# Left operands of the seven products made two products ahead, and the input's quarter sums from a float32 copy

## The chip, the cores and the metric

The kernel runs on one core of a Trainium2 chip, as one launch. The engines of a core run their own instruction queues in order and meet through semaphores: TensorE (PE: matmuls; PEld: its loads of the left operand), VectorE (DVE), ScalarE (ACT), GpSimd (POOL) and SyncE (SP), which issues the weight loads. The metric is the device time of one execution in microseconds (us). Three runs of the kernel before took 1692.21 us in the median, 1684.16 to 1693.19.

## The reference

One inference step of a two-layer decoder trunk over 544 tokens: 512 tokens of one prompt and 8 sequences of 4 tokens. Layer 0 is a convolution module and a SwiGLU feed-forward network (FFN). Layer 1 is sparse attention, over keys and values projected once, and a second SwiGLU FFN. Each part is normalised, then scaled and shifted by a vector per sequence. The change is in the FFN of layer 1:

```python
def swiglu(h, w_gate, w_up, w_down):
    return (jax.nn.silu(h @ w_gate) * (h @ w_up)) @ w_down

shift, scale, gate = ada_modulation(c, w_ada[l, 1], b_ada[l, 1])
h = rmsnorm(x, norm_g[l, 1]) * (1 + scale) + shift
x = x + gate * swiglu(h, w_gate[l], w_up[l], w_down[l])
```

Here h is 544 x 1024, `w_gate` and `w_up` are 1024 x 2816, `w_down` is 2816 x 1024, all float32.

## The kernel before, in words

Activations lie with features on the 128 partitions and tokens in columns: `h` is 8 feature tiles of 128 x 544. float32 accuracy comes from splitting each operand into a high part, rounded to the type float32r, and a low part, the rest. A product of two operands takes three matmuls: high x high, high x low and low x high. ScalarE makes the high part of a weight tile (`whi`) by a cast, VectorE the low part (`wlo`) by a subtraction. `whi` and `wlo` are rings of four buffers, each of four 128 x 128 tiles, and the raw weights (`raw`) a ring of four, each of eight. A buffer comes free when the last instruction that reads it is done.

The 22 output tiles ("units") of the FFN's hidden width are done in three thirds, of 8, 8 and 6 units. In each third the gate and up products are made, then multiplied by the third's part of `w_down` and added to x. In the second FFN (line 1698, `start` is given) there are three kinds of units. Units 0 and 1 (`EARLY`) multiply the unnormalised x, so that they can start before the norm is known. Then `modulated` (line 520) makes the high and low parts of the true h, and units 2 and 3 use them plainly: we call these the whole units. From unit 4 on (`SEVEN`), units go in pairs through `seven_units` (line 881), which calls `seven` (line 222) twice, for gate and up.

One call of `seven` multiplies a 256-row block of weights (two units, two halves of the input features) by two halves of the tokens with seven half-size products instead of eight (a 2 x 2 block scheme with sums of blocks on both sides). The left operands are, in program order, a11, the sums s1, s2, the block a12, the sums s4, s3, and a22. `seven_weights` (line 198) is a generator that makes each of them when it is asked for. The right operands are three quarters of h, and four quarter sums T ("t1" to "t4"), made once for all calls by `sums_of_halves` (line 255). One product ("term", line 232) is 12 matmuls of 272 columns. Terms of one call gather in three PSUM areas (`p1`, `p2`, `p3`), of which ScalarE copies out intermediate values (lines 240, 242, 245) before the next term adds to them, and VectorE adds results (lines 247, 249, 251). The last term of a call is done only after the next call's second (`earlier`), so calls are chained. There are 9 pairs, 18 calls: 2 pairs in the first third, 4 in the second, 3 in the last.

`sums_of_halves` rebuilds h as high + low in float32 (line 261, into the ring `ht` of three buffers, which the whole units' SiLU and other temporaries use as well), forms four combinations of 272 columns (lines 264 to 267, tile `su`), and splits them into T's high part (line 269, ScalarE) and low part (line 270, VectorE). It is called for four pairs of feature tiles, two after unit 2 and two after unit 3 (line 856). GpSimd makes low parts of the hidden activations (lines 855 and 904).

The order of instructions on each engine is chosen when the kernel is built. A scheduler walks the program with its own estimate of times and takes ready instructions by their place in the program, so an operation that is written earlier tends to stand earlier. At run time each engine follows that order strictly.

Of the kernel before, what the change touches and what calls it, by code (L numbers as in the profile page):

```python
# [7 lines left out]
F32 = mybir.dt.float32  # L8
# [6 lines left out]
P = 128  # L15
D = 1024
KT = D // P
SEQ = 512
# [94 lines left out]
class Kernel:  # L113
# [83 lines left out]

    def seven_weights(self, src, pool):


        add = lambda out, x, y: self.v.tensor_tensor(out=out, in0=x, in1=y, op=ALU.add)  # L201
        a = self.wp.tile([P, KT, P], F32, name="raw", bufs=4)
        b = self.wp.tile([P, KT, P], F32, name="raw", bufs=4)
        s24 = pool.tile([P, 2, 4, P], F32, name="s24", bufs=2)
        s13 = pool.tile([P, 2, 4, P], F32, name="s13", bufs=1)
        self.sy.dma_start(a, src[:, :, :P])
        self.sy.dma_start(b, src[:, :, P:])
        av, bv = [t.rearrange("p (k c) n -> p c k n", c=2) for t in (a, b)]
        a11, a12, a22, s1, s3 = av[:, 0], av[:, 1], bv[:, 1], s13[:, 0], s13[:, 1]
        add(s1, bv[:, 0], a22)  # L210
        yield self.split4(a11)
        yield self.split4(s1)
        add(s24[:, 0], s1, a11)
        yield self.split4(s24[:, 0])
        yield self.split4(a12)
        add(s24[:, 1], s24[:, 0], a12)
        yield self.split4(s24[:, 1])
        add(s3, a11, bv[:, 0])
        yield self.split4(s3)
        yield self.split4(a22)  # L220

    def seven(self, src, X, pool, c1, c22, earlier):

# [5 lines left out]
        p1, p2 = pg[:, 0, :n], pg[:, 1, :n]  # L229
        ws = self.seven_weights(src, pool)  # L230

# [22 lines left out]

    def sums_of_halves(self, hi, lo, T, i, pool):

        v, s = self.v, self.s
        n = TOK // 2
        x = [self.tp.tile([P, TOK], F32, name="ht", bufs=3) for _ in range(2)]
        for c in range(2):  # L260
            v.tensor_tensor(out=x[c], in0=hi[:, 2 * i + c, :TOK].bitcast(F32), in1=lo[:, 2 * i + c, :TOK].bitcast(F32), op=ALU.add)
        (b11, b12), (b21, b22) = [(t[:, :n], t[:, n:]) for t in x]
        t = [pool.tile([P, TOK], F32, name="su", bufs=2).rearrange("p (a n) -> p a n", a=2) for _ in range(2)]
        v.tensor_tensor(out=t[0][:, 0], in0=b11, in1=b12, op=ALU.subtract)
        v.scalar_tensor_tensor(out=t[0][:, 1], in0=b22, scalar=-1.0, in1=t[0][:, 0], op0=ALU.mult, op1=ALU.subtract)
        v.tensor_tensor(out=t[1][:, 0], in0=b22, in1=b12, op=ALU.subtract)
        v.scalar_tensor_tensor(out=t[1][:, 1], in0=t[0][:, 1], scalar=-1.0, in1=b21, op0=ALU.mult, op1=ALU.subtract)
        for a in range(2):
            s.copy(T[0][:, i, 2 * a:2 * a + 2], t[a])
            v.tensor_tensor(out=T[1][:, i, 2 * a:2 * a + 2], in0=t[a], in1=T[0][:, i, 2 * a:2 * a + 2].bitcast(F32), op=ALU.subtract)  # L270

    def quarters(self, hi, lo, T):
        n = TOK // 2
        at = lambda x, c, a: lambda i: x[:, 2 * i + c, a * n:(a + 1) * n]
        X = {k: (at(hi, c, a), at(lo, c, a)) for k, c, a in (("11", 0, 0), ("21", 1, 0), ("22", 1, 1))}
        of = lambda x, j: lambda i: x[:, i, j]
        X.update({f"t{j + 1}": (of(T[0], j), of(T[1], j)) for j in range(4)})
        return X
# [240 lines left out]

    def modulated(self, m, rstd):  # L520

        for f in range(KT):
            self.modulated_prompt(m, f, rstd)
            if f == 0:
                self.modulated_decode(m, 0, KT, rstd)

    def modulated_prompt(self, m, f, rstd):
        a, b = self.mod[:, m, 1], self.mod[:, m, 0]
        t = self.tp.tile([P, TOK], F32, name="ht", bufs=3)
        self.v.scalar_tensor_tensor(out=t[:, :SEQ], in0=self.x[:, f, :SEQ], scalar=a[:, f, 0:1], in1=rstd[:, :SEQ],  # L530
                                    op0=ALU.mult, op1=ALU.mult)
        self.s.activation(self.h_hi[:, f, :SEQ], t[:, :SEQ], AF.Identity, bias=b[:, f, 0:1])
        self.v.scalar_tensor_tensor(out=self.h_lo[:, f, :SEQ], in0=t[:, :SEQ], scalar=b[:, f, 0:1],
                                    in1=self.h_hi[:, f, :SEQ].bitcast(F32), op0=ALU.add, op1=ALU.subtract)

    def modulated_decode(self, m, f0, f1, rstd):
# [9 lines left out]
        self.s.copy(self.h_hi[:, f0:f1, SEQ:], ts)  # L546
        self.v.tensor_tensor(out=self.h_lo[:, f0:f1, SEQ:], in0=ts, in1=self.h_hi[:, f0:f1, SEQ:].bitcast(F32), op=ALU.subtract)  # L547

    def unscaled_shift(self, m, hi, lo):
# [244 lines left out]
    def ffn(self, l, pool, between=(), done=lambda f: None, start=None):  # L794
# [15 lines left out]
        if start is not None:  # L810
            sums = self.tc.tile_pool(name="sums", bufs=1, side="right", reuse_waits="tile")
            sp = sums.__enter__()
            T = [sp.tile([P, 4, 4, TOK // 2], F32R, name=f"T{c}") for c in range(2)]
            X = self.quarters(self.h_hi, self.h_lo, T)
        for lo, hi in ((0, 8), (8, 16), (16, FT)):
            for j in range(lo, hi):
                if start is not None and j >= SEVEN:
                    if (j - lo) % 2 == 0:
                        left = self.seven_units(j, lo, gs, us, X, sp, pool, left, a_hi, a_lo)
                        for _ in range(4):  # L820
                            next(between, None)
                    continue
# [3 lines left out]
                if start is not None and j == EARLY:  # L826
                    self.modulated(m, rstd)
                if early:
# [23 lines left out]
                while units and not (early and j < EARLY - 1):  # L852
                    i, sg = j - lo + 1 - len(units), units.pop(0)
                    s.copy(a_hi[:, i], sg)  # L854
                    self.last_pool = g.tensor_tensor(out=a_lo[:, i], in0=sg, in1=a_hi[:, i].bitcast(F32), op=ALU.subtract).ins  # L855
                if start is not None and EARLY <= j < EARLY + 2:
                    for i in range(2):
                        self.sums_of_halves(self.h_hi, self.h_lo, T, 2 * (j - EARLY) + i, sp)
                next(between, None)
# [20 lines left out]

    def seven_units(self, j, lo, gs, us, X, sp, pool, left, a_hi, a_lo):

        v, s, g = self.v, self.s, self.g
        n = TOK // 2
        sg = [pool.tile([P, TOK], F32, name="early", bufs=2 * EARLY) for _ in range(2)]
        p1, last = self.seven(gs[:, :, j * P:(j + 2) * P], X, sp, sg[0], sg[1][:, n:], left)
        s.activation(sg[0], sg[0], AF.Silu)
# [8 lines left out]

        s0, s1 = self.tp.tile([P, TOK], F32, name="ht", bufs=3), sp.tile([P, TOK], F32, name="su", bufs=2)[:, :n]
        q1, end = self.seven(us[:, :, j * P:(j + 2) * P], X, sp, s0, s1, gates)
        v.tensor_tensor(out=sg[0], in0=sg[0], in1=s0, op=ALU.mult)
# [832 lines left out]
```

## Time and profile before

| | |
|---|---|
| median of three runs | 1692.21 us |
| the profiled execution | 1690.65 us |
| its span, first to last instruction | 1688.9 us |
| mean granted TensorE clock over it | 0.976 of full speed |
| TensorE busy | 1584.2 us, 94% |
| VectorE busy | 1000.5 us, 59% |
| ScalarE busy | 645.8 us, 38% |
| GpSimd busy | 231.9 us, 14% |

The second FFN's norm and whole units begin near 1281 us, the first call of `seven` near 1322 us. Its thirds end with down products near 1382 to 1426, 1523 to 1567 and from 1639 us on. In the timelines a matmul's end is modelled: matmuls overlap, and at full pace one begins about every 0.126 us while each shows 0.29 us. So time that is lost is read from start to start. "x2" is two instructions that the view merged.

### The profile page before, as it was taken

How to read it: one execution, taken by the hardware profiler on the slowest of the kernel's cores; microseconds unless marked ns; L12 is line 12 of the kernel's file. 1: busy time of each engine (PE TensorE's matmuls, PEld its weight loads, DVE VectorE, ACT ScalarE, POOL GpSimd, SP SyncE). 2: the span in 40 equal slices, each digit the busy share in tenths (PEclk: the TensorE clock that was granted, in tenths of full speed). 3: DMA queues.
4: the chain of work that ended last, by engine and by line, in shares of the span. 5: the costliest groups of instructions: out<-in, count | busy, mean ns of one | idle time of the engine just before them, and what ended most of it. 6: DMA issues, size and time to landing. Idle time of an engine off the chain costs nothing. (4 is left out here: it accounts for less than half of the span.)

```text
span 1688.9 us, 31583 instructions
## 1 busy us (share of the span) xinstructions
PE 1584.2 (94%) x12591; PEld 1388.1 (82%) x12591; DVE 1000.5 (59%) x2167; ACT 645.8 (38%) x1328; POOL 231.9 (14%) x267
## 2 busy tenths in 40 slices
PE   6889869999999999989999899999999899999997
PEld 3689337989988999989978677655699899999997
DVE  1799645473325554422657544876757865874766
ACT  4322106232122222123545332756644442552554
POOL 2146420021221111001110000000011310010010
PEclk9999978999999999999999999999999899999999
DMA  7745875374389999952379896847023372333231
GB/s 228 186 138 132 199 236 174 103 237 138 120 217 333 335 338 324 253 158 69 106 243 282 253 281 189 249 125 233 25 76 100 114 226 82 91 101 88 77 90 63
DMA packets 315326, 296.05 MB, mean 175 GB/s; under 512 B 15843, under 2 KB 275053, under 8 KB 310939
## 3 DMA queue, kind: packets, MB, share of 16 engines
q1 hardware_dynamic: 304507, 237.24, 47.6%
q0 software_dynamic: 10368, 56.56, 10.5%
q8 instruction: 99, 1.62, 0.4%
q14 instruction: 48, 0.39, 0.1%
q10 hardware_dynamic: 304, 0.23, 0.1%
HBM read 257.39 MB, written 45.76 MB: 179 GB/s over the span
## 5 line engine op out<-in xcount | busy, mean ns | idle before, releaser
L168 ACT CAST whi<-raw 128x512 fp32r<-128x512 f32 (+1 forms) x306 | 184.0, 609 | 549.1 <-PE g L184 344.5
L169 DVE TENSOR_TENSOR wlo<-raw,whi 128x512 fp32r<-128x512 f32 (+1 forms) x306 | 212.0, 696 | 228.5 <-ACT whi L168 222.9
L182 PE MATMUL g<-h_hi,whi 128*128 128x256 f32 (+1 forms) x808 | 236.7, 294 | 19.6 <-DVE un L649 8.8
L184 PE MATMUL g<-h_hi,whi 128*128 128x272 f32 (+3 forms) x808 | 239.4, 297 | 0.7 <-ACT h_hi L546 0.7
L184 PE MATMUL g<-h_lo,whi 128*128 128x272 f32 (+3 forms) x808 | 239.3, 296 | 0.4 <-DVE h_lo L547 0.4
L184 PE MATMUL g<-h_hi,wlo 128*128 128x272 f32 (+3 forms) x808 | 239.4, 296 | 0.0
L182 PE MATMUL g<-h_lo,whi 128*128 128x256 f32 (+1 forms) x808 | 233.3, 289 | 0.0
L182 PE MATMUL g<-h_hi,wlo 128*128 128x256 f32 (+1 forms) x808 | 233.0, 288 | 0.0
L182 PEld LDWEIGHTS g<-h_hi,whi 128*128 128x128 f32 x808 | 154.7, 192 | 33.7 <-issue 13.2
L184 PEld LDWEIGHTS g<-h_hi,whi 128*128 128x128 f32 x808 | 154.7, 192 | 4.6 <-issue 3.5
L182 PEld LDWEIGHTS g<-h_lo,whi 128*128 128x128 f32 x808 | 155.1, 192 | 3.7 <-issue 3.5
L184 PEld LDWEIGHTS g<-h_hi,wlo 128*128 128x128 f32 x808 | 154.5, 191 | 3.4 <-issue 3.4
L184 PEld LDWEIGHTS g<-h_lo,whi 128*128 128x128 f32 x808 | 154.2, 191 | 2.9 <-issue 2.1
L182 PEld LDWEIGHTS g<-h_hi,wlo 128*128 128x128 f32 x808 | 155.0, 192 | 1.3 <-issue 1.0
L182 PE MATMUL g<-a_hi,whi 128*128 128x256 f32 (+1 forms) x372 | 107.1, 288 | 6.2 <-ACT a_hi L854 2.7
L184 PE MATMUL g<-a_hi,wlo 128*128 128x288 f32 (+1 forms) x372 | 110.5, 297 | 0.0
L184 PE MATMUL g<-a_hi,whi 128*128 128x288 f32 (+1 forms) x372 | 110.2, 297 | 0.0
L184 PE MATMUL g<-a_lo,whi 128*128 128x288 f32 (+1 forms) x372 | 109.8, 295 | 0.0
L182 PE MATMUL g<-a_hi,wlo 128*128 128x256 f32 (+1 forms) x372 | 105.4, 284 | 0.7 <-DVE wlo L169 0.7
L182 PE MATMUL g<-a_lo,whi 128*128 128x256 f32 (+1 forms) x372 | 105.0, 282 | 0.9 <-POOL a_lo L855 0.9
L237 PE MATMUL g<-T,whi 128*128 128x272 f32 x432 | 84.0, 290 | 2.2 <-ACT early L240 2.2
L182 PEld LDWEIGHTS g<-a_hi,whi 128*128 128x128 f32 x372 | 70.7, 190 | 11.7 <-ACT whi L168 4.5
(467 smaller groups left out, 3428.1 us busy)
## 6 DMA issues: line engine op xcount, KB each, us to landing
raw<-in_w_ada_dram SPq DMA_DIRECT2D x96, 512.0 KB
raw<-in_w_gate_dram SPq DMA_DIRECT2D x44, 512.0 KB
raw<-in_w_up_dram SPq DMA_DIRECT2D x44, 512.0 KB
raw<-in_w_down_dram SPq DMA_DIRECT2D x32, 512.0 KB
raw<-in_w_pw_dram SPq DMA_DIRECT2D x24, 512.0 KB
kt_d<-ktr SPq DMA_DIRECT2D x96, 128.0 KB
kt<-kt_d SPq DMA_DIRECT2D x24, 512.0 KB
raw<-in_w_kv_dram SPq DMA_DIRECT2D x20, 512.0 KB
```

Of the source, the lines that this page charges most:

```text
L168: self.s.copy(hi[:, :b - a], raw[:, a:b])
L169: self.v.tensor_tensor(out=lo[:, :b - a], in0=raw[:, a:b], in1=hi[:, :b - a].bitcast(F32), op=ALU.subtract)
L182: self.te.matmul(pg[:, 0, :split], a, b[:, i, :split], start=st, stop=sp)
L184: self.te.matmul(pg[:, 1, :tokens - split], a, b[:, i, split:tokens], start=st, stop=sp)
L237: self.te.matmul(out, a[:, i], b(i), start=first and i == 0 and j == 0, stop=i == 3 and j == 2, skip_group_check=not first)
```

## The change

The generator `seven_weights` now runs over all weight blocks of a third (`srcs`), and `ahead` draws from it so that, whenever a product takes its operand, the two after it have already been written into the program, across calls too. The sums lie in a ring `s4` of three buffers, in place of `s13` and `s24`, and each is written directly behind the product before it.

`modulated` takes a function `whole`. For each feature tile ScalarE then also writes h in float32, without rounding (a second activation of 512 columns and a copy of 32), into a tile of the same ring `s4`. `sums_of_halves` takes that tile and forms the four combinations in place, so lines 261 and the `ht` tiles are gone from it, and it splits all four at once, 1088 columns wide. The first call of it is written before feature tile 6 of `modulated`, the other three after unit 2. T's columns are stored in another sequence (`quarters`).

```diff
-    def seven_weights(self, src, pool):
-        add = lambda out, x, y: self.v.tensor_tensor(out=out, in0=x, in1=y, op=ALU.add)
...
-        s24 = pool.tile([P, 2, 4, P], F32, name="s24", bufs=2)
-        s13 = pool.tile([P, 2, 4, P], F32, name="s13", bufs=1)
...
+    def seven_weights(self, srcs, pool):
+        def sums(x, y):
+            out = pool.tile([P, 4, TOK // 2], F32, name="s4", bufs=3).rearrange("p a n -> p (a n)")[:, :4 * P].rearrange("p (k n) -> p k n", k=4)
+            self.v.tensor_tensor(out=out, in0=x, in1=y, op=ALU.add)
+            return out
+
+        for src in srcs:
+            raws = [self.wp.tile([P, KT, P], F32, name="raw", bufs=4) for _ in range(2)]
+            for i, raw in enumerate(raws):
+                self.sy.dma_start(raw, src[:, :, i * P:(i + 1) * P])
+            (a11, a12), (a21, a22) = [[r.rearrange("p (k c) n -> p c k n", c=2)[:, c] for c in range(2)] for r in raws]
+            yield self.split4(a11)
+            s1 = sums(a21, a22)
+            yield self.split4(s1)
+            s2 = sums(s1, a11)
+            yield self.split4(s2)
+            yield self.split4(a12)
+            s4 = sums(s2, a12)
+            yield self.split4(s4)
+            yield self.split4(sums(a11, a21))
+            yield self.split4(a22)
+
+    def ahead(self, it, n):
+        made = []
+        for x in it:
+            made.append(x)
+            if len(made) > n:
+                yield made.pop(0)
+        yield from made
...
-    def sums_of_halves(self, hi, lo, T, i, pool):
+    def sums_of_halves(self, x, T, i):
...
-        x = [self.tp.tile([P, TOK], F32, name="ht", bufs=3) for _ in range(2)]
-        for c in range(2):
-            v.tensor_tensor(out=x[c], in0=hi[:, 2 * i + c, :TOK].bitcast(F32), in1=lo[:, 2 * i + c, :TOK].bitcast(F32), op=ALU.add)
...
-        for a in range(2):
-            s.copy(T[0][:, i, 2 * a:2 * a + 2], t[a])
-            v.tensor_tensor(out=T[1][:, i, 2 * a:2 * a + 2], in0=t[a], in1=T[0][:, i, 2 * a:2 * a + 2].bitcast(F32), op=ALU.subtract)
+        q = [x[:, j] for j in range(4)]
+        v.tensor_tensor(out=q[0], in0=q[0], in1=q[1], op=ALU.subtract)
+        v.tensor_tensor(out=q[1], in0=q[3], in1=q[1], op=ALU.subtract)
+        v.scalar_tensor_tensor(out=q[3], in0=q[3], scalar=-1.0, in1=q[0], op0=ALU.mult, op1=ALU.subtract)
+        v.scalar_tensor_tensor(out=q[2], in0=q[3], scalar=-1.0, in1=q[2], op0=ALU.mult, op1=ALU.subtract)
+        s.copy(T[0][:, i], x)
+        v.tensor_tensor(out=T[1][:, i], in0=x, in1=T[0][:, i].bitcast(F32), op=ALU.subtract)
...
-    def modulated(self, m, rstd):
+    def modulated(self, m, rstd, whole=None):
...
+            if whole:
+                out = whole(f)
+                self.s.activation(out[:, :SEQ], t[:, :SEQ], AF.Identity, bias=self.mod[:, m, 0, f, 0:1])
+                self.s.copy(out[:, SEQ:], ts[:, f])
...
+            xs = []
+
+            def whole(f):
+                if f == KT - 2:
+                    self.sums_of_halves(xs[0], T, 0)
+                if f % 2 == 0:
+                    xs.append(sp.tile([P, 4, TOK // 2], F32, name="s4", bufs=3))
+                return xs[-1].rearrange("p (c a) n -> p c (a n)", c=2)[:, f % 2]
         for lo, hi in ((0, 8), (8, 16), (16, FT)):
+            if start is not None:
+                ws = self.ahead(self.seven_weights((m[:, :, j * P:(j + 2) * P] for j in range(max(lo, SEVEN), hi, 2) for m in (gs, us)), sp), 2)
...
-                    self.modulated(m, rstd)
+                    self.modulated(m, rstd, whole)
...
-                if start is not None and EARLY <= j < EARLY + 2:
-                    for i in range(2):
-                        self.sums_of_halves(self.h_hi, self.h_lo, T, 2 * (j - EARLY) + i, sp)
+                if start is not None and j == EARLY:
+                    for i in range(1, 4):
+                        self.sums_of_halves(xs[i], T, i)
```

Up to `modulated` of the second FFN every engine's order is the same as before. Three places behind it are shown. Lines of the changed kernel are shifted: 245 is the matmul of a term (237 before), 539 the low half of h (533), 267 to 270 the quarter combinations, 272 T's low part, 203 a sum of weight blocks (201), 257 and 255 the PSUM adds (249, 247), 913 the multiply by an up product (895).

VectorE, before the last low half of h, which is the last row of both pieces (`h_lo`; the number behind `s` tells tiles of the ring `s4` apart). Before:

```order
L584 SCALAR_TENSOR_TENSOR early<-g,rstd 128x544
L533 SCALAR_TENSOR_TENSOR h_lo<-ht,mod,h_hi 128x512
L169 TENSOR_TENSOR wlo<-raw,whi 128x512
L590 TENSOR_TENSOR early<-early,wb 128x32
L838 SCALAR_TENSOR_TENSOR early<-early,wb 128x512
L533 SCALAR_TENSOR_TENSOR h_lo<-ht,mod,h_hi 128x512
```

Now:

```order
L536 SCALAR_TENSOR_TENSOR ht<-x,mod,rstd 128x512
L268 TENSOR_TENSOR s_13955<-s_13955 128x272
L272 TENSOR_TENSOR T_13629<-s_13929,T_13628 128x1088
L169 TENSOR_TENSOR wlo<-raw,whi 128x512
L270 SCALAR_TENSOR_TENSOR s_13942<-s_13942 128x272
L539 SCALAR_TENSOR_TENSOR h_lo<-ht,mod,h_hi 128x512
L598 TENSOR_TENSOR early<-early,wb 128x32
L856 SCALAR_TENSOR_TENSOR early<-early,wb 128x512
L269 SCALAR_TENSOR_TENSOR s_13955<-s_13955 128x272
L539 SCALAR_TENSOR_TENSOR h_lo<-ht,mod,h_hi 128x512
```

Four rows of the second piece (L268, L272, L270, L269) make quarter sums, which stood behind the last low half before. From the first `ht` of `modulated` to the last low half VectorE now has eleven quarter combinations, one low part of T and one weight copy more than before. On TensorE, unit 2 asks for that last low half after 88 of its 96 matmuls (gate and up together), where it asked after 62.

TensorE, at a seam between two calls (`g_15300` and `g_15296` are the old call's PSUM tile, `g_15422` and `g_15434` the new call's, `t_15423` its s1 product). Before:

```order
L237 MATMUL g_15300<-h_hi_103,wlo_15362 128x272
L237 MATMUL g_15422<-h_hi_103,whi_15431 128x272
L237 MATMUL g_15422<-h_lo_104,whi_15431 128x272
L237 MATMUL t_15423<-T0_13628,whi_15448 128x272
L237 MATMUL t_15423<-T1_13629,whi_15448 128x272
L237 MATMUL g_15422<-h_hi_103,wlo_15432 128x272
```

Now:

```order
L245 MATMUL g_15296<-h_hi_103,wlo_15332 128x272
L245 MATMUL g_15434<-h_hi_103,whi_15407 128x272
L245 MATMUL g_15434<-h_lo_104,whi_15407 128x272
L245 MATMUL g_15434<-h_hi_103,wlo_15408 128x272
L245 MATMUL g_15434<-h_hi_103,whi_15407 128x272
L245 MATMUL g_15434<-h_lo_104,whi_15407 128x272
```

The two matmuls of the new s1 product that stood between the second and third matmul of the new a11 product are gone from there; s1 now follows after twelve matmuls of a11 and twelve of the old call's s3.

VectorE, at the second pair's seam between gate and up: `wlo_15672` and `wlo_15648` are the low copy of s3, `wlo_15706` and `wlo_15686` that of the new a11. Before:

```order
L195 TENSOR_TENSOR wlo_15672<-s13_15564,whi_15671 128x512
L201 TENSOR_TENSOR s13_15701<-raw_15699 128x512
L895 SCALAR_TENSOR_TENSOR early_15299<-g_15422,early_15299 128x272
L201 TENSOR_TENSOR s13_15701<-raw_15698,raw_15699 128x512
L195 TENSOR_TENSOR wlo_15689<-raw_15562,whi_15688 128x512
L201 TENSOR_TENSOR s24_15700<-s13_15701,raw_15698 128x512
L249 TENSOR_TENSOR early_15557<-t_15560,early_15557 128x272
L195 TENSOR_TENSOR wlo_15706<-raw_15698,whi_15705 128x512
```

Now:

```order
L195 TENSOR_TENSOR wlo_15648<-s4_15645,whi_15647 128x512
L913 SCALAR_TENSOR_TENSOR early_15295<-g_15434,early_15295 128x272
L203 TENSOR_TENSOR s4_15763<-s4_15714,raw_15681 128x512
L195 TENSOR_TENSOR wlo_15665<-raw_15541,whi_15664 128x512
L257 TENSOR_TENSOR early_15571<-t_15574,early_15571 128x272
L195 TENSOR_TENSOR wlo_15686<-raw_15681,whi_15685 128x512
```

The sum that stood between the low copy of s3 and the multiply (L895, now L913) is gone from there, and so are the two sums before the PSUM add (L249, now L257); one sum of the next call has come in its place.

## Rows read from the trace of the kernel before

**Rows 1.** Busy time by stretch: stretch, length, busy us (instructions) per engine, granted clock, DMA

```profile
1290.00:1310.00 20.00, 20.00 (x159) 20.00 (x159) 18.15 (x34) 9.78 (x17) 3.60 (x3) 1.00 0.44 132
...
1320.00:1330.00 10.00, 7.67 (x47) 6.91 (x45) 9.62 (x18) 4.62 (x9) 4.29 (x1) 0.83 0.50 159
1330.00:1340.00 10.00, 7.45 (x33) 6.78 (x32) 8.19 (x14) 4.12 (x8) 1.92 (x2) 0.66 0.49 156
...
1321.90:1340.40 18.50, 13.59 (x65) 12.01 (x64) 16.69 (x30) 7.58 (x15) 6.20 (x2) 0.72 0.37 114
```

**Rows 2.** TensorE's waits, 1300 to 1650 us: total us, times, longest

```profile
PE t L237 <- ACT whi L194: 4.6, 14, 0.3
PE g L237 <- DVE wlo L195: 2.7, 6, 0.5
PE g L237 <- ACT early L240: 2.2, 1, 2.2
PE g L182 <- ACT whi L168: 1.9, 3, 0.6
```

**Rows 3.** Timeline, TensorE, first call: start, us, operation, [idle before <-releaser]

```profile
1321.89 0.29 PE L237 MATMUL g<-h_hi,whi 128*128 128x272 f32 x1
...
1324.02 0.29 PE L237 MATMUL t<-T,wlo 128*128 128x272 f32 x1
...
1326.48 0.82 PE L237 MATMUL g<-T,whi 128*128 128x272 f32 x2 [2.17 <-ACT early L240]
...
1333.89 0.59 PE L237 MATMUL t<-h_hi,whi 128*128 128x272 f32 x1 [0.67 <-ACT early L242]
...
1340.40 0.28 PE L237 MATMUL g<-h_hi,wlo 128*128 128x272 f32 x1
```

**Rows 4.** Timeline, TensorE, two seams of the second third

```profile
1445.30 0.29 PE L237 MATMUL g<-h_lo,whi 128*128 128x272 f32 x1
1445.92 0.52 PE L237 MATMUL t<-T,whi 128*128 128x272 f32 x2 [0.33 <-ACT whi L194]
...
1456.47 0.29 PE L237 MATMUL g<-h_lo,whi 128*128 128x272 f32 x1
1457.09 0.52 PE L237 MATMUL t<-T,whi 128*128 128x272 f32 x2 [0.33 <-ACT whi L194]
1458.05 0.40 PE L237 MATMUL g<-h_hi,wlo 128*128 128x272 f32 x1 [0.45 <-DVE wlo L195]
```

**Rows 5.** Timeline, ScalarE and VectorE, before and in the first call

```profile
1319.19 0.62 ACT L847 ACTIVATE ht<-g 128x544 f32<-128x544 f32 x1 [2.75 <-POOL a_lo L855]
...
1320.38 0.72 DVE L270 TENSOR_TENSOR T<-su,T 128x544 fp32r<-128x544 f32 x1 [2.45 <-ACT T L269]
...
1331.68 1.51 DVE L270 TENSOR_TENSOR T<-su,T 128x544 fp32r<-128x544 f32 x2
```

**Rows 6.** Timeline, the engines around the whole units, 1283 to 1310 us

```profile
1283.77 1.33 ACT L532 ACTIVATE h_hi<-ht,mod 128x512 fp32r<-128x512 f32 x2
...
1294.64 1.88 DVE L533 SCALAR_TENSOR_TENSOR h_lo<-ht,mod,h_hi 128x512 fp32r<-128x512 f32 x1
...
1297.55 0.29 PE L182 MATMUL g<-h_hi,whi 128*128 128x272 f32 x1
...
1301.86 0.74 DVE L533 SCALAR_TENSOR_TENSOR h_lo<-ht,mod,h_hi 128x512 fp32r<-128x512 f32 x1
...
1306.98 1.35 DVE L261 TENSOR_TENSOR ht<-h_hi,h_lo 128x544 f32<-128x544 f32 x2
...
1309.45 0.43 DVE L264 TENSOR_TENSOR su<-ht 128x272 f32<-128x272 f32 x1
```

**Rows 7.** Timeline, ScalarE, GpSimd and VectorE at a long seam

```profile
1454.93 0.62 ACT L194 CAST whi<-raw 128x512 fp32r<-128x512 f32 x1
...
1455.12 1.38 POOL L904 TENSOR_TENSOR a_lo<-early,a_hi 128x544 fp32r<-128x544 f32 x1 [4.56 <-PE t L237]
...
1455.41 1.64 DVE L201 TENSOR_TENSOR s<-s,raw 128x512 f32<-128x512 f32 x1
```

More of the change, by code (lines that the diff above doesn't have):

```diff
@@ L196, in split4, with seven @@
         return hi, lo
-    def seven_weights(self, src, pool):
-        add = lambda out, x, y: self.v.tensor_tensor(out=out, in0=x, in1=y, op=ALU.add)
-        a = self.wp.tile([P, KT, P], F32, name="raw", bufs=4)
-        b = self.wp.tile([P, KT, P], F32, name="raw", bufs=4)
-        s24 = pool.tile([P, 2, 4, P], F32, name="s24", bufs=2)
-        s13 = pool.tile([P, 2, 4, P], F32, name="s13", bufs=1)
[L206 to L222, printed above, removed]
+    def seven_weights(self, srcs, pool):
[25 more added lines that the diff above has]
+        yield from made
+    def seven(self, ws, X, c1, c22, earlier):
         v, s = self.v, self.s
@@ L229, in seven @@
         p1, p2 = pg[:, 0, :n], pg[:, 1, :n]
-        ws = self.seven_weights(src, pool)
         def term(out, w, x, first):
@@ L253, in seven @@
         return p1, lambda: term(p1, w, "t4", False)
-    def sums_of_halves(self, hi, lo, T, i, pool):
+    def sums_of_halves(self, x, T, i):
         v, s = self.v, self.s
-        n = TOK // 2
-        x = [self.tp.tile([P, TOK], F32, name="ht", bufs=3) for _ in range(2)]
-        for c in range(2):
-            v.tensor_tensor(out=x[c], in0=hi[:, 2 * i + c, :TOK].bitcast(F32), in1=lo[:, 2 * i + c, :TOK].bitcast(F32), op=ALU.add)
[L262 to L267, printed above, removed]
-        for a in range(2):
-            s.copy(T[0][:, i, 2 * a:2 * a + 2], t[a])
-            v.tensor_tensor(out=T[1][:, i, 2 * a:2 * a + 2], in0=t[a], in1=T[0][:, i, 2 * a:2 * a + 2].bitcast(F32), op=ALU.subtract)
+        q = [x[:, j] for j in range(4)]
[5 more added lines that the diff above has]
+        v.tensor_tensor(out=T[1][:, i], in0=x, in1=T[0][:, i].bitcast(F32), op=ALU.subtract)
     def quarters(self, hi, lo, T):
@@ L276, in quarters @@
         of = lambda x, j: lambda i: x[:, i, j]
-        X.update({f"t{j + 1}": (of(T[0], j), of(T[1], j)) for j in range(4)})
+        X.update({f"t{j + 1}": (of(T[0], q), of(T[1], q)) for j, q in enumerate((0, 3, 1, 2))})
         return X
@@ L518, in rstd_of_x @@
         return self.rsqrt_mean(acc, True)
-    def modulated(self, m, rstd):
+    def modulated(self, m, rstd, whole=None):
         for f in range(KT):
-            self.modulated_prompt(m, f, rstd)
+            t = self.modulated_prompt(m, f, rstd)
             if f == 0:
-                self.modulated_decode(m, 0, KT, rstd)
+                ts = self.modulated_decode(m, 0, KT, rstd)
+            if whole:
+                out = whole(f)
+                self.s.activation(out[:, :SEQ], t[:, :SEQ], AF.Identity, bias=self.mod[:, m, 0, f, 0:1])
+                self.s.copy(out[:, SEQ:], ts[:, f])
     def modulated_prompt(self, m, f, rstd):
@@ L534, in modulated_prompt @@
                                     in1=self.h_hi[:, f, :SEQ].bitcast(F32), op0=ALU.add, op1=ALU.subtract)
+        return t
     def modulated_decode(self, m, f0, f1, rstd):
@@ L547, in modulated_decode @@
         self.v.tensor_tensor(out=self.h_lo[:, f0:f1, SEQ:], in0=ts, in1=self.h_hi[:, f0:f1, SEQ:].bitcast(F32), op=ALU.subtract)
+        return ts
     def unscaled_shift(self, m, hi, lo):
@@ L818, in ffn @@
                     if (j - lo) % 2 == 0:
-                        left = self.seven_units(j, lo, gs, us, X, sp, pool, left, a_hi, a_lo)
+                        left = self.seven_units(j, lo, ws, X, sp, pool, left, a_hi, a_lo)
                         for _ in range(4):
@@ L879, in ffn, with seven_units @@
             pass
-    def seven_units(self, j, lo, gs, us, X, sp, pool, left, a_hi, a_lo):
+    def seven_units(self, j, lo, ws, X, sp, pool, left, a_hi, a_lo):
         v, s, g = self.v, self.s, self.g
@@ L885, in seven_units @@
         sg = [pool.tile([P, TOK], F32, name="early", bufs=2 * EARLY) for _ in range(2)]
-        p1, last = self.seven(gs[:, :, j * P:(j + 2) * P], X, sp, sg[0], sg[1][:, n:], left)
+        p1, last = self.seven(ws, X, sg[0], sg[1][:, n:], left)
         s.activation(sg[0], sg[0], AF.Silu)
@@ L895, in times @@
             v.scalar_tensor_tensor(out=out, in0=x, scalar=-1.0, in1=out, op0=ALU.mult, op1=ALU.mult)
-        s0, s1 = self.tp.tile([P, TOK], F32, name="ht", bufs=3), sp.tile([P, TOK], F32, name="su", bufs=2)[:, :n]
-        q1, end = self.seven(us[:, :, j * P:(j + 2) * P], X, sp, s0, s1, gates)
+        s0, s1 = self.tp.tile([P, TOK], F32, name="ht", bufs=3), sp.tile([P, n], F32, name="su", bufs=2)
+        q1, end = self.seven(ws, X, s0, s1, gates)
         v.tensor_tensor(out=sg[0], in0=sg[0], in1=s0, op=ALU.mult)
```

## The prediction

> **What bounds the kernel now.** I read four views, in this order. The busy time by stretch says which engine sets the pace: from 1290 to 1310 us TensorE has a matmul in flight all 20 us, 159 of them (one per 0.126 us) at a granted clock of 1.00, while VectorE is busy 18.15 us and ScalarE 9.78 us [rows 1]. So in the second FFN a wait of TensorE is lost time, and VectorE, with little room, is the likeliest cause of one. The same view finds the bad place: in 1320 to 1340 us only 47 and 33 matmuls are counted per 10 us, and the clock is 0.83 and 0.66 of 2.4 GHz, on its way to the 1.2 GHz level [rows 1]. The list of TensorE's waits from 1300 to 1650 us names the partners: 14 short waits for the high copy of a left operand (ScalarE, L194), 6 for a low copy (VectorE, L195), and a few large ones for quarter sums T and for a copy out of PSUM [rows 2]. The timelines price both kinds.
>
> *The first call of the seven products.* It begins at 1321.89 us. TensorE goes on with T products until 1324.02, stands until 1326.48, then takes T matmuls one by one as they come, and starts the next term at 1333.89; at 1340.40 it is back at full pace [rows 3]. 63 matmuls begin between 1321.89 and 1340.40 (the x65 of the window also counts two from before [rows 1]). At 0.126 us they need 7.9 us; they took 18.5. Lost: 10.6 us, waiting and half clock together. The cause is upstream: the last low part of T ends at 1331.68 + 1.51 = 1333.2 us. VectorE itself had stood 2.45 us before an earlier T for ScalarE, and ScalarE 2.75 us before its L847, the SiLU that needs a tile of the "ht" ring, for GpSimd [rows 5]. Sums, SiLU outputs and GpSimd's operand share that ring of three.
>
> *The seams.* Where one call follows another, two matmuls of the new s1 product stand in TensorE's order in the middle of the new a11 product, and s1's high copy is late. There are two sizes. Short: 1445.30 to 1445.92 is 0.62 us where 0.126 is due, 0.49 lost. Long, where the low copy of a11 is late too: 1456.47 to 1457.09 loses 0.49, and 1457.09 to 1458.05 holds two matmuls (0.25) and loses 0.71, together 1.20 [rows 4]. With the counts 14 and 6 [rows 2] that is 8 x 0.49 + 6 x 1.20 = 11.1 us.
>
> **The change part by part.** *Quarter sums from a float32 copy.* Removed: 8 adds of 544 columns (two take 1.35 us [rows 6], some 5.2 us of VectorE) and their use of the ht ring, so L847 has no sums to queue behind there. Kept: 16 quarter operations of 272 columns. The casts and low parts of T become 4 + 4 of 1088 columns instead of 8 + 8 of 544. A 1088-wide operation isn't in the trace: one 544-wide, 0.7 us, is the floor, two, 1.35, the ceiling; I take 1.3, since the work per column stays. Added on ScalarE: 8 activations of 512 columns (two take 1.33 us [rows 6]), 5.3 us, and 8 copies of 32 columns, not in these rows, between nothing and 0.66 each; I take 0.15, since they are a sixteenth as wide, so some 6.5 us in all. ScalarE has room for them (9.78 of 20 us busy [rows 1]) beneath the early units' matmuls. Alone they cost nothing; without that cover they would cost their 6.5 us.
>
> What they delay is the question. VectorE now does 11 quarter operations, one 1088-wide low part and one more weight copy before the last low half of the activations. At full durations (0.43, 1.3 and 0.68 us) that is 6.7 us; since the next operation starts some 0.08 us before the one ahead of it ends, nearer 5.7. That half ended at 1301.86 + 0.74 = 1302.6 us [rows 6], so now at 1308.3 to 1309.3. TensorE's unit 2 begins at 1297.55 [rows 6] and, in its new order, asks for that half after 88 matmuls: 1297.55 + 88 x 0.126 = 1308.6 us. The cover is just spent: between 0.3 us early and 0.7 us late. I take 0, and for the range 0 to 4 us, three more delays like the low half of 1.88 us instead of 0.74 at 1294.64 [rows 6].
>
> After that half VectorE has 18 operations to the end of the last T part: five of 272, eight of 512, three of 1088, one of 544 and one of 32 columns, 5 x 0.43 + 8 x 0.68 + 3 x 1.3 + 0.7 + 0.2 = 12.4 us at full durations. That ends at 1320.7 to 1321.7 us, and TensorE asks for T twelve matmuls after 1321.89, at 1323.4. With 1.7 us in hand the 10.6 us go whole, the half clock with them; if the hand is spent by blocks, some 4 us of them stay.
>
> *Operands two products ahead.* At a seam the order now has all 24 matmuls of a12 and a11 in a row, then twelve of s3, and only then s1: s1's operand gets 24 more matmuls (3 us) after the slot for it is free. The 8 x 0.49 and the 6 x 0.49 go. What is late next is a11's low copy, since all four slots of each ring stay in use: a11's high copy can start only when the s4 product has freed a slot, as at 1454.93 [rows 7], and its third matmul wants the low copy at about 1456.6. VectorE's order has only a PSUM add between, so it can start at 1455.5 and end at 1456.2. But at the 6 long seams GpSimd runs: it began at 1455.12 for 1.38 us, and the VectorE sum that began at 1455.41 took 1.64 us, ending 0.55 after GpSimd [rows 7]; a low copy that starts at 1455.5 in its place ends at about 1457.1 and costs 0.5 us. GpSimd's operation hangs on the last up product, and VectorE's multiply for it now has one sum fewer ahead of it (0.6 us), so the overlap is partly gone: 0.3 us at each of 6, 1.8 us (bounds 0 and 6 x 0.71).
>
> The Trainium skill, page "SBUF — State Buffer", section "Who interferes with whom", says that a VectorE instruction with two SBUF inputs and a GpSimd instruction that reads SBUF share an exclusive lock, and that whichever issues first keeps it for the whole instruction. The trace agrees at 1455.41 (1.64 us). By the rule each of the six would cost the full 0.5 us, and the sum would be 1.2 us smaller.
>
> *The rest.* SyncE issues the same loads in the same sequence, both halves of a pair together; each waits for a slot that a low copy frees, and those copies come no later than before, so nothing is charged. The three waits, 1.9 us, for down weights (L168) [rows 2] use the same four slots and are left as they are. Until the second FFN every engine's order is the same.
>
> *Sum.* 10.6 + 11.1 - 1.8 - 0 = 19.9 us. From the profiled execution, 1690.65 us (span 1688.9 and 1.75 around it), to 1670.8. The median of the runs is 1.6 us above that execution, and the runs spread over 9 us, so I say 1671.
>
> **The rivals.** (1) *The low halves come late*: the sums stand in front of what TensorE wants next, and unit 2 stops in their place. For it: the cover computed above is about zero, and VectorE is busy 18.15 of 20 us. Against: TensorE's order was rearranged to ask later. Price: the 4 us bound, and, as in the windows at 0.83 and 0.66, some 2.7 us of half clock for two dozen matmuls: 1671 + 6.7, about 1678.
>
> (2) *T stays late*: VectorE, unbroken from 1282 us on, loses the 1.7 us in hand to GpSimd blocks, and half of the 10.6 us remains: 1676.
>
> (3) *The change does not do what it says at the seams*: four slots hold the live operands, so an operand "two ahead" waits for its slot anyway, and the seams lose their 11.1 us in another order. For it: the s1 copies of the trace before waited for a slot, not for their sums. Against: the two misplaced matmuls are gone from TensorE's order. Price: 1690.65 - 10.6, about 1680.
>
> (4) *The other side: ScalarE's queue*. Copies out of PSUM (L240, L242, L245) stand behind casts that wait for a slot; with casts further ahead TensorE waits for the copy. It has happened once: 2.17 us for L240 at 1326.48 [rows 3]. If each of the other 17 calls paid that, 37 us would stand against 20, 1708 us; it decides from 1.2 us a call. Against it: in the new ScalarE order the cast ahead of a copy waits for a product that ends no later than the copy's own.
>
> **How the numbers follow.** Forecast 0.60, own range 1665 to 1677 (what stays at the seams, and what the low halves take); (1) 0.14, (2) 0.10, (3) 0.12, (4) 0.04. The 8-in-10 range is 1663 to 1683: below, nothing is left at the seams, the down waits go too (2 us), and the runs spread 4 us; above, it takes in rivals (1) to (3). A measurement of this kernel tells a change from none at about 0.5%, 8.5 us, that is below 1683.7: all of the forecast, nearly all of (1) and (2) and four fifths of (3): faster 0.86, same 0.10, slower 0.04.
>
> **What would show it.** Right: 1320 to 1340 us at clock 1.00 with some 159 matmuls; no wait for T or L240's copy; the 14 waits for the high copy gone, and at most six of some 0.3 to 0.5 us for a low copy. Rival (1) shows as a gap before the last twelve matmuls of unit 2, near 1308 us; (2) as waits for T; (3) as waits for the high copy, about 14 still; (4) as waits for L248, L250 or L253 in most calls. The forecast is wrong if the sum of TensorE's waits after 1297 us is above 10 us, or if the time moved before 1282 us, where the order is unchanged.

## The result, and the profile after

The changed kernel took 1674.07 us in the median of 6 runs (1668.86 to 1678.53), beside 1692.70 us for the kernel before in 6 runs on the same chip (1684.16 to 1702.27). The ratio is 0.9885, with a 95% interval of 0.9839 to 0.9931. Beside two later experiments it was run again: 0.9894 (0.986 to 0.9929) and 0.9916 (0.9891 to 0.9942). In each of these two one run of the changed kernel took far longer than the rest (4003 and 2151 us), as did one of the kernel before beside `low_later_again` (1937 us); the ratios leave these out. The prediction was 1671, from 1663 to 1683.

A run's time moves by several us for reasons that lie before the change. So the experiments are read by a *stage*: from the first matmul of unit 2 to the end of the span. Unit 2 began at 1297.55 us before and at 1300.09 after, 2.54 us later. That shift isn't the change's: 2.52 us of it are there at 1200 us, and the orders first differ near 1283 us, on ScalarE. In three profiles of the changed kernel unit 2 began at 1300.09, 1302.69 and 1305.23, while the stage took 371.31, 371.31 and 371.17 us. The stage shrank from 391.35 to 371.31, by 20.04 us (a span is given to 0.1 us, so a stage is good to 0.05 us). The table cuts it by the starts of TensorE's first matmuls: units 2 and 3, then from each third's first term of seven products to its first down product (us):

| kernel | units 2, 3 | first third | second | third | stage |
|---|---|---|---|---|---|
| before | 24.34 | 51.74 | 87.91 | 64.85 | 391.35 |
| changed | 25.10 | 39.83 | 82.88 | 61.31 | 371.31 |
| `before_ring3` | 24.33 | 48.62 | 82.92 | 61.32 | 379.41 |
| `one_buffer` | 25.10 | 41.46 | 86.85 | 64.15 | 380.30 |
| `ahead0` | 25.10 | 40.41 | 82.85 | 61.27 | 371.84 |
| `own_ring` | 25.11 | 46.39 | 82.90 | 61.34 | 377.87 |
| `late_low` | 29.86 | 39.72 | 82.85 | 61.27 | 376.67 |
| `low_halves` | 25.11 | 41.21 | 82.86 | 61.27 | 372.93 |
| `tiny_low` | 25.10 | 39.31 | 81.53 | 60.40 | 367.85 |
| `low_vector` | 25.10 | 39.88 | 83.00 | 61.37 | 371.17 |
| `low_later` | 25.10 | 40.46 | 81.75 | 60.57 | 370.89 |
| `low_later_again` | 25.11 | 41.54 | 81.75 | 60.57 | 371.40 |

What follows the third third's terms, the last down products and the output, is part of the stage and took 56.7 us in all three profiles of the changed kernel, but 57.4 in `late_low` and `low_later`. In their last 8 us the granted clock was 0.50, the 1.2 GHz level, where the changed kernel's profile has 0.70. So a difference below 0.8 us is read from the columns of the table and not from the whole stage.

The busy time by stretch, with the columns of [rows 1], shows the first call (it starts at 1325.19 now):

```profile
1310.00:1320.00 10.00, 9.52 (x76) 9.30 (x75) 10.00 (x16) 5.48 (x9) 5.72 (x4) 1.00 0.74 254
1320.00:1330.00 10.00, 10.00 (x82) 10.00 (x81) 8.42 (x12) 5.14 (x10) 1.60 (x2) 1.00 0.53 164
1330.00:1340.00 10.00, 10.00 (x81) 10.00 (x81) 7.32 (x13) 5.73 (x12) 0.00 (x0) 1.00 0.35 107
```

Where [rows 1] had 47 and 33 matmuls at clocks of 0.83 and 0.66, there are 82 and 81 at 1.00. TensorE's waits from 1297 us to the end, as in [rows 2]:

```profile
PE g L182 <- ACT whi L168: 1.9, 3, 0.6
PE t L154 <- ACT ht L1552: 1.7, 1, 1.7
PE g L245 <- DVE wlo L195: 0.9, 5, 0.2
PE g L182 <- DVE x L620: 0.5, 1, 0.5
PE g L182 <- ACT ht L865: 0.5, 1, 0.5
```

The 14 waits for a high copy and that for L240 [rows 2] are gone, and so are those for T, which the same view of before lists as:

```profile
PE t L237 <- ACT T L269: 1.1, 1, 1.1
PE t L237 <- DVE T L270: 0.9, 2, 0.7
```

Five for a low copy stay, and one is new, for the SiLU L865. The timeline of the whole units and the first call, the answer to [rows 3, 5, 6]:

```profile
1309.42 0.74 DVE L539 SCALAR_TENSOR_TENSOR h_lo<-ht,mod,h_hi 128x512 fp32r<-128x512 f32 x1
...
1321.55 1.28 DVE L272 TENSOR_TENSOR T<-s,T 128x1088 fp32r<-128x1088 f32 x1
...
1311.26 0.29 PE L182 MATMUL g<-h_lo,whi 128*128 128x272 f32 x1
...
1312.91 0.39 PE L182 MATMUL g<-h_hi,whi 128*128 128x272 f32 x1 [0.48 <-ACT ht L865]
...
1326.70 0.41 PE L245 MATMUL t<-T,whi 128*128 128x272 f32 x2
```

The last low half ends at 1310.16, 1.1 us before TensorE asks for it (1311.26). T is complete at 1322.83, 3.9 us before it is asked for (1326.70). A long seam, the answer to [rows 4, 7]:

```profile
1445.07 0.63 ACT L194 CAST whi<-raw 128x512 fp32r<-128x512 f32 x1
...
1445.07 1.38 POOL L922 TENSOR_TENSOR a_lo<-early,a_hi 128x544 fp32r<-128x544 f32 x1 [4.62 <-PE t L245]
...
1445.36 0.44 DVE L257 TENSOR_TENSOR early<-t,early 128x272 f32<-128x272 f32 x1
1445.72 1.27 DVE L195 TENSOR_TENSOR wlo<-raw,whi 128x512 fp32r<-128x512 f32 x1
...
1447.05 0.39 PE L245 MATMUL g<-h_hi,wlo 128*128 128x272 f32 x1 [0.17 <-DVE wlo L195]
```

The low copy of the new a11 takes 1.27 us beside GpSimd's operation, ends 0.54 us after it, and TensorE takes its third matmul 0.34 us late and the next 0.11 late: 0.45 us at five seams, some 0.26 at two of the first third, 2.8 us in all.

### The profile page after: what moved, and what is told of

The parts are those of the page before. It is cut to its first block, busy times and chain, and to the rows that moved or that the text cites. A ratio compares the mean times of both kernels' runs of the same rounds, so it can differ in the third digit from the quotient of the medians.

```text
span 1671.4 us, 31595 instructions
## 1 busy us (share of the span) xinstructions
PE 1569.4 (94%) x12591; PEld 1381.3 (83%) x12591; DVE 997.7 (60%) x2155; ACT 649.7 (39%) x1340; POOL 225.7 (14%) x267
## 3 DMA queue, kind: packets, MB, share of 16 engines
q0 software_dynamic: 10368, 56.56, 10.6%
## 4 chain that ended last, share of the span: by engine, by line
PE 73%; DMA 10%; DVE 9%; SPq 3%; issue 3%; ACT 2%; POOL 0%; ACTq 0%; DVEq 0%
PE g L184 23%; PE g L182 22%; PE g L245 6%; PE t L154 3%; PE t L987 3%; PE o L1468 3%; PE t L245 2%; DMA raw<-in_w_ada_dram 2%; PE a L443 2%; DVE y L732 1%; DMA raw<-in_w_down_dram 1%; SPq L1372 1%; PE t L1317 1%; DMA w<-in_w_phi_dram 1%; DVE wlo L195 1%
```

## Experiments

*What moved the seams.* Built with a look-ahead of 0, 1, 2 or 3, the changed kernel has the same instructions in the same order on every engine. So the look-ahead can't be the cause. What else changed at the seams is where the sums lie: s1 and s3 of a call shared the one buffer `s13`, so that a call's s1 could be written only after s3 of the call before had been split; in the ring `s4` each sum has its own. Three runs tell this apart. The first gives the kernel before a ring of three and nothing else:

```diff
-        s24 = pool.tile([P, 2, 4, P], F32, name="s24", bufs=2)
-        s13 = pool.tile([P, 2, 4, P], F32, name="s13", bufs=1)
+        s1, s2, s4, s3 = [pool.tile([P, 4, P], F32, name="sm", bufs=3) for _ in range(4)]
```

> The kernel before, with one thing changed: the sums s1, s2, s4, s3 lie in a ring of three single buffers instead of s13 (one buffer shared by s1 and s3) and s24. No look-ahead, no float32 copy. The stage is the time from unit 2's first matmul to the end of the span: 391.35 us before, 371.31 after. Theory R (the ring of the sums moved the seams): the seams gain what they gained in the changed kernel, 11.1 - 2.8 = 8.3 us, the first call still loses its 10.6; stage 382 to 384, run about 1684. Theory P (the prediction's: operands written two products ahead moved them): nothing changes, stage 390 to 392, 14 waits for the high copy stay, run about 1692.

Stage 379.41; median 1683.44 of 10 runs, ratio 0.9964 (0.9944 to 0.9984). The second and third thirds shrank to 82.92 and 61.32, those of the changed kernel, without look-ahead. TensorE's waits keep the first call's and lose the high copies:

```profile
PE t L236 <- ACT T L268: 3.1, 1, 3.1
...
PE t L236 <- DVE T L269: 1.6, 2, 0.8
PE g L236 <- DVE wlo L195: 1.0, 6, 0.2
```

Theory P falls. The gain, 11.9 us, is 3.6 above theory R's 8.3, and so the stage lies below its range: 1.7 of it lies in the first call (0.4 at such a seam, the rest in T's waits), 0.3 behind the last terms, and each of the 14 seams had cost 0.1 us more than priced in [rows 4], since the matmul behind the two late ones was late as well. The second run undoes only the separate buffers in the changed kernel:

```diff
...
+            if one:
+                out = pool.tile([P, 4, P], F32, name="s13", bufs=1)
...
-            s1 = sums(a21, a22)
+            s1 = sums(a21, a22, True)
...
-            yield self.split4(sums(a11, a21))
+            yield self.split4(sums(a11, a21, True))
```

> The changed kernel, with one thing undone: s1 and s3 share a ring of one buffer. Look-ahead of two and float32 copy stay. Theory R: the two s1 matmuls stand again in the middle of a11, some 14 waits for the high copy come back; stage 371.3 + 8.3 = 379.6, 378 to 382, run about 1682. Theory P: the look-ahead is there, so the seams stay gone: stage 371 to 372.5, run about 1674.

Stage 380.30; median 1683.99, ratio 0.9969 (0.9941 to 0.9997). Two s1 matmuls stand in the middle of a11 again, and the waits are back, with the look-ahead in place. (From here to the changed kernel the three thirds shrink by 8.4 us, where they shrank by 11.6 from before to `before_ring3`: at the long seams a11's low copy is 0.35 us late here, 0.71 before, and the first call has little left to gain here, as told below.)

```profile
PE t L248 <- ACT whi L194: 5.0, 15, 0.3
```

The third sets the look-ahead to 0 (`sp), 2)` becomes `sp), 0)`).

> The changed kernel with the look-ahead set from 2 to 0, ring and float32 copy kept. Theory R: the orders of the engines are those of the changed kernel, stage 371.3 within 1 us. Theory P: the seams come back, stage 379 to 382 with some 14 waits for the high copy.

Stage 371.84, 1671.03 us in one run, with the changed kernel's order on every engine in the trace: as theory R says, though it's in effect one more run of the changed kernel.

*What made T late.* The kernel before with the ring of three, and two buffers for the rebuilt h:

```diff
-        x = [self.tp.tile([P, TOK], F32, name="ht", bufs=3) for _ in range(2)]
+        x = [pool.tile([P, TOK], F32, name="hx", bufs=2) for _ in range(2)]
```

> The kernel before with the ring of three for the sums, and with h rebuilt as high + low as before, but in two buffers of its own instead of the shared ring ht. No float32 copy: the eight adds of 544 columns stay on VectorE. Theory S (the shared ring made T late): T comes some 5.2 us of adds later than in the changed kernel, where it had 3.9 us in hand, so it is about 1.3 us late; first call loses 1 to 4 us, stage 372.5 to 375.5, run about 1676. Theory W (the work of the adds made T late, the float32 copy is what helps): the first call still loses some 8 to 11 us, stage 380 to 384.

Stage 377.87; median 1678.18 of 7 runs, ratio 0.9919 (0.9893 to 0.9945): between the theories, nearer to W. We count what TensorE loses in the 18.5 us from the first call's begin, against 0.1265 us a matmul: 10.5 before, 8.8 with the ring of three, 6.6 here, nothing in the changed kernel. Here VectorE doesn't stand still once from unit 2's begin to the end of T (it did for 4.3 us before), yet T ends 34.0 us after that begin, against 35.6 before and 22.7 changed. The timelines of TensorE, VectorE and GpSimd:

```profile
1327.26 0.39 PE L236 MATMUL t<-T,whi 128*128 128x272 f32 x1 [2.13 <-ACT T L268]
...
1327.76 2.30 DVE L269 TENSOR_TENSOR T<-su,T 128x544 fp32r<-128x544 f32 x2
...
1324.32 5.16 POOL L854 TENSOR_TENSOR a_lo<-ht,a_hi 128x544 fp32r<-128x544 f32 x1 [10.86 <-ACT a_hi L853]
```

In that stretch VectorE has 6 adds (3.8 us), 4 more quarter operations (1.4) and 8 more copies, sums and multiplies of later work that stand ahead of the last T (5.0) than in the changed kernel. So the shared ring was worth 2.2 of the 10.5 us. The other 6.6 go with the float32 copy, and not with the ring of the sums: `one_buffer`, which has the copy but not the separate buffers, loses 0.4 us in the same 18.5. Which part of the copy does it isn't shown: the 6 adds are gone, but the quarter operations also begin sooner and the later work stands behind T, and no run parts the three.

*What a late low half costs.* The last low half of h is written twice:

```diff
-        self.v.scalar_tensor_tensor(out=self.h_lo[:, f, :SEQ], in0=t[:, :SEQ], scalar=b[:, f, 0:1],
+        for _ in range(2 if f == KT - 1 and m == 3 else 1):
+            self.v.scalar_tensor_tensor(out=self.h_lo[:, f, :SEQ], in0=t[:, :SEQ], scalar=b[:, f, 0:1],
```

> The changed kernel, with the last low half of h (feature tile 7) written a second time. On VectorE the repeat stands one 1088-wide low part and four shorter operations behind the first, so it ends some 3.2 us later, while TensorE's order is unchanged. In the changed kernel the half ended 1.1 us before TensorE asked for it. Theory C (the cover is spent at 1.1 us and lateness is paid one for one): TensorE waits 2.1 us for it after 88 matmuls of unit 2; T has 3.9 us in hand and stays in time, the clock stays; the stage grows from 371.3 to 373.4, 373 to 374.5. Theory D (rival 1's price, a wait of this kind brings half clock with it): stage 375 to 378. Theory E (there was more cover than the trace shows): no wait, stage 371 to 372.

Stage 376.67, 5.36 more, in theory D's range. Of that, units 2 and 3 took 4.76; 0.8 lies at the very end of the span, behind the last down products, and isn't the edit's, since `low_later` has the same there. GpSimd held the repeat up (1.63 us instead of 0.74), so TensorE waited 3.0 us instead of 2.1; then the clock was below full. Timelines, and the window's columns as above:

```profile
1321.67 1.63 DVE L540 SCALAR_TENSOR_TENSOR h_lo<-ht,mod,h_hi 128x512 fp32r<-128x512 f32 x1
...
1323.36 0.39 PE L182 MATMUL g<-h_lo,whi 128*128 128x272 f32 x1 [3.00 <-DVE h_lo L540]
```

```profile
1320.00:1330.00 10.00, 6.52 (x37) 6.08 (x37) 9.24 (x14) 4.96 (x8) 4.50 (x4) 0.83 0.50 160
```

From start to start the wait lost 3.16 us; the other 1.6 of the 4.76 are the clock. That is still theory D and not C: without the 0.8 the stage would be 375.9.

*What is left at the seams.* First the second unit's high and low parts in two halves, the first before the last up product; beside it the changed kernel again:

```diff
...
         parts(0)
+        parts(1, n)
...
-            parts(1)
+            parts(1, 0, n)
```

> The changed kernel, with the second unit's high and low parts made in two halves of 272 columns, the first of them before the last up product, so that GpSimd's operation at the seam is half as wide. Theory G (what is left at the seams is VectorE's low copy of a11 held up by GpSimd's 1.38 us operation): five losses of 0.45 and two of 0.28 go, stage 371.3 - 2.8 = 368.5, 368 to 369.5, no wait for L195 left. Theory H (the low copy of a11 is late for its slot, whatever GpSimd does): the five waits stay, stage 371 to 372.

> The changed kernel once more, beside the one before it in this list, on one chip: stage 371.3 to 371.9, about 19 us faster than the kernel before.

Stages 372.93 and 371.31, medians 1673.87 and 1675.65, ratios 0.9888 (0.986 to 0.9915) and 0.9894 (0.986 to 0.9929). The waits stay (6, 1.0 us), so theory G as it stands falls, but H isn't shown by that. GpSimd and VectorE at a seam:

```profile
1443.98 0.67 POOL L922 TENSOR_TENSOR a_lo<-early,a_hi 128x272 fp32r<-128x272 f32 x1 [2.09 <-issue]
1446.68 1.20 POOL L922 TENSOR_TENSOR a_lo<-early,a_hi 128x272 fp32r<-128x272 f32 x1 [2.03 <-ACT a_hi L921]
...
1444.03 1.17 DVE L203 TENSOR_TENSOR s<-s,raw 128x512 f32<-128x512 f32 x1
...
1447.62 0.80 DVE L195 TENSOR_TENSOR wlo<-raw,whi 128x512 fp32r<-128x512 f32 x1
```

The first half took 0.48 us from a sum (1.17 for 0.69), the second 0.12 from the low copy: 0.60 together, as before. Two runs ask whether any time that GpSimd takes in the seam arrives there. In `tiny_low` the low part's width is 32 columns (`n = 32 if i else TOK`); in `low_vector` VectorE makes it (`e = v if i else g`).

> The changed kernel, with GpSimd's low part for the second unit of each pair made for 32 of its 544 columns only (the other columns of that part are left out), so that GpSimd hardly runs at the seams. Theory G2 (VectorE has no gap there, so any time that GpSimd takes from it anywhere in the seam arrives at a11's low copy): the five losses of 0.45 and two of 0.28 go, stage 371.3 - 2.8 = 368.5, 368 to 369.3, no wait for L195. Theory H (the low copy of a11 is late for its slot, whatever GpSimd does): five waits of 0.17 stay, stage 371 to 372.

> The changed kernel, with the same low part made by VectorE instead of GpSimd. Theory G2: the 0.6 us that GpSimd takes from VectorE become 0.6 us of VectorE's own, so the waits for a11's low copy stay at about 0.2 us, and a T product that now stands earlier in TensorE's order at every second seam may add waits for a high copy; stage 371 to 375. Theory H gives the same for the low copies. Only a stage of 368 to 369.5 would say that it was the sharing itself, not VectorE's load.

Stages 367.85 and 371.17 (one run each, 1671.50 and 1678.02 us); no wait for L195 in the first, six of 0.2 us in the second. The three thirds of `tiny_low` are 2.8 us shorter than the changed kernel's, as forecast. Its stage is 0.7 more below, and that of `low_vector` 0.4, since the last down products stand in another order there and the wait for L620 is gone. G2 holds: VectorE has no gap at the seam, and 0.6 us more there costs TensorE some 0.45, whoever takes it. In `tiny_low` VectorE's timeline has room behind the low copy:

```profile
1447.02 0.69 DVE L195 TENSOR_TENSOR wlo<-raw,whi 128x512 fp32r<-128x512 f32 x1
1447.97 0.44 DVE L255 TENSOR_TENSOR early<-g,early 128x272 f32<-128x272 f32 x1 [0.25 <-PE g L245]
```

So a version that leaves nothing out holds the high part back, and GpSimd with it, to where VectorE has gaps:

```diff
...
+        if self.late:
+            z = sp.tile([P, 1], F32, name="z", bufs=2)
+            s.activation(z, sg[0][:, :1], AF.Copy, scale=0.0)
+            self.late(z)
+            self.late = None
...
+                s.activation(a_hi[:, j - lo + i], sg[i], AF.Identity, bias=z)
...
-            parts(1)
+            self.late = lambda z=None: parts(1, z)
```

> The changed kernel, with the second unit's high part (and so GpSimd's low part behind it) held back until ScalarE has done the next pair's first SiLU, by a bias of zero made from that SiLU's result. Nothing is left out; the orders of TensorE, VectorE and GpSimd are unchanged, ScalarE gets 6 tiny operations. Theory G2 (VectorE has no gap at the seam, but has some 0.5 us of gaps a few us later): GpSimd's 1.38 us fall where VectorE has gaps, the waits for a11's low copy go, stage 367.9 to 369, about 3 us below the changed kernel. Theory I (GpSimd's operation costs VectorE as much wherever it runs, and TensorE pays): stage 371 to 372 with other waits of 0.2 to 0.5 us, five or six of them.

> The changed kernel once more on the same chip as the one before it in this list: stage 371.3 to 371.9.

> The version with GpSimd's low part held back, once more: its first profile lost 0.7 us more than the changed kernel in the first third, where VectorE waited 2.32 us for a weight load, and gained 1.9 us in the second and third. Theory G2: the late load is not the edit's; without it the stage is 371.2 - 1.9 = 369.3, 369 to 370. Theory I: the loss in the first third comes with the edit, stage 370.5 to 371.5 again.

Medians 1671.17 and 1672.85, ratios 0.9877 (0.9851 to 0.9902) and 0.9868 (0.983 to 0.9906); the changed kernel beside the first 0.9916. The five waits are gone, and the second and third thirds took 81.75 and 60.57 in both, 1.85 us below the changed kernel. But the stages are 370.89 and 371.40, against 371.17, since the first third took 0.7 and 1.8 us longer than there, and what follows the last terms 0.8 and 0.3. In the first third of both, VectorE had waited over 2.3 us for a weight load. The second profile, on VectorE, ScalarE and TensorE:

```profile
1325.00 0.69 DVE L203 TENSOR_TENSOR s<-raw 128x512 f32<-128x512 f32 x1 [2.39 <-DMA raw<-in_w_up_dram]
...
1326.36 0.65 ACT L873 CAST a_hi<-ht 128x544 fp32r<-128x544 f32 x1 [2.13 <-DVE ht L867]
...
1327.43 0.38 ACT L248 COPY early<-g 128x272 f32<-128x272 f32 x1
...
1327.87 0.52 PE L245 MATMUL g<-T,whi 128*128 128x272 f32 x2 [1.07 <-ACT early L248]
```

A sum waits for a load, the multiply behind it is late, the cast that needs it holds ScalarE, and the copy out of PSUM stands behind that cast. (In the first profile it is a later load, of a gate block, and the loss lies at the add L259 and at the first seam.) By its stage the first run lies between the two theories' ranges and the second in theory I's. Against theory I, the loss lies in both profiles before the first instruction that the edit moves, where every engine's order is the changed kernel's; `ahead0`, in the order of the changed kernel, has the same wait of TensorE as above (0.4 us, first third 40.41), and `low_halves` has 0.9. But the gate load made VectorE wait 2.32 and 2.20 us with the edit, and 1.16 to 1.66 in four profiles of the changed kernel's order, so two profiles don't settle it. What sets when those loads land wasn't tried. So 1.85 us are shown in two thirds; the whole runs, whose intervals overlap, don't tell this version from the changed kernel.

## Why the prediction was right, and where not

*The sum.* 19.9 us were forecast for the stage, 20.04 were measured. By places: units 2 and 3 lost 0.76, the first third gained 11.91, the second 5.03, the third 3.54, the rest 0.32. That the sum came so close is partly luck, since its terms were off and nearly cancelled: the seams had cost 1.4 more than 11.1 (14 times 0.1), 2.8 instead of 1.8 stayed there, and units 2 and 3, charged with nothing, took 0.76. The profiled execution is 2.3 us above the forecast because unit 2 began 2.54 us later, a shift from before the first order that differs.

*The first call.* The 10.6 us went whole, the half clock with them. The step "the cause is upstream", which named the two stalls at the shared ring, was right only in part: without the sharing 6.6 us stay lost and VectorE never stands. The larger cause is the length of VectorE's queue ahead of the last T, which the float32 copy shortens; the prediction had listed the adds that it removes (5.2 us) but not as the reason, and how much of the 6.6 is theirs stays open.

*Operands two products ahead.* Here the mechanism was wrong. The prediction gave the seams to the look-ahead ("s1's operand gets 24 more matmuls"). The runs give them to the ring of the sums; the look-ahead does nothing. Its reading that the s1 copies "waited for a slot, not for their sums" describes the run, but the order in which they stood had been set when the kernel was built, and `one_buffer` shows that the shared buffer set it. TensorE's new order was read rightly, so the price came out although the reason didn't, which is luck. That the change doesn't do what it says was thus true of one half of it, without rival (3)'s price.

*What stays at the seams.* 1.8 us were taken, 2.8 measured; the mechanism was right, the mitigation ("the overlap is partly gone: 0.3 us") wrong. The Trainium skill's lock (page "SBUF — State Buffer", section "Who interferes with whom"), by which each of six would cost 0.5 us, comes nearer, with 0.45 at five and some 0.26 at two. The rows agree with it twice: the two-input low copy waited for GpSimd's end, while L257, which takes one input from PSUM, ran its 0.44 us beside it.

*Low halves and T.* Between 0.3 early and 0.7 late was forecast, 1.1 early measured; for T 1.7 us in hand, 3.9 measured (the end was 0.4 us sooner than the earlier bound, and units 2 and 3 took 0.76 longer). Rival (1) stayed out by about a microsecond, and `late_low` shows its price: 4.76 us in units 2 and 3 for a wait of 3.16, 1.5 times the wait, where 1.7 times had been sized (6.7 for 4). The 1088-wide low part took 1.28 us for the 1.3 taken.

*Not foreseen.* Unit 3's begin waits 0.48 us for the SiLU L865, which stands behind casts on ScalarE; from start to start that is 0.74 us, all that units 2 and 3 lost. Rival (4)'s mechanism occurs, but at most once per run, from 0 to 1.07 us, when a load is late.

*Signs and chances.* TensorE's waits behind 1297 us add up to 5.5 us, below the 10 that would have shown the forecast wrong. Its other sign was badly chosen: the time did move before 1282 us, by 2.5 us, but unit 2's begin moves by up to 5.1 us between the three profiles of the changed kernel. The 0.86 for "faster" doesn't follow from the chances that it names; they add up to some 0.93.

## What to carry to other kernels

Where a builder orders instructions, a ring with too few buffers can put an instruction in the wrong place without showing as a wait on that buffer; look for two operands that share a buffer before writing anything ahead, and compare the built order with and without each part of a change. When the engine that feeds the bottleneck has no gap, price an operation by the time it takes from that engine, wherever it runs: here halving it gained nothing, and moving it gained only where it ended up beside a gap. Compare a late stage by its own span, since the run before it can move by more than the change is worth.

## What the runs showed of the hardware

GpSimd's operation of 544 columns took between 1.14 and 6.56 us. The longest, in the kernel before, began at 1312.59 us and is the one that L847 waited for [rows 5]. VectorE's operations ran beside it at their usual lengths, one behind the other, until 1317.93, and it ended 1.22 us after that, about the 1.14 that it takes at the least. So GpSimd seems to have waited through all of them. In `own_ring` it took 5.16 us, and there the last two low parts of T took 2.30 us together, where two 544-wide adds take 1.35 [rows 6]: both engines can pay at such a place. And the same weight load, in the same order, made VectorE wait 0.84 us in the changed kernel's profile and 2.39 in `low_later_again`; a copy out of PSUM behind it turned that into 1.07 us of TensorE.
